# A hybrid decoder layer on one core: where the shift, scale and gate vectors are made

## The chip, the core and the metric

The kernel runs on one core of a Trainium2 chip. The metric is the device time of one launch in microseconds (us). TensorE (PE) multiplies matrices into PSUM; VectorE (DVE), ScalarE (ACT) and GpSimd (POOL) work element by element; SyncE (SP) issues nearly all DMAs. Each engine takes its own instructions strictly in the order that was fixed when the program was built, and waits on semaphores for the others. So does SP: a DMA that has to wait holds up those queued behind it.

## The reference

One decoder layer on a sequence of 1024 tokens of width 1024, in float32. A conditioning vector c gives six modulation vectors; the change is about four of them.

```python
c_act = jax.nn.silu(c)
mod = c_act @ w_ada[i] + b_ada[i]                    # (1, 6 * 1024)
sh1, sc1, g1, sh2, sc2, g2 = jnp.split(mod, 6)
h = rmsnorm(x, pre_mix_g[i]) * (1.0 + sc1) + sh1
q, k, v, u = jnp.split(h @ w_in[i], split_pts, axis=-1)
attn = sliding_window_attention(q, k, v, attn_sinks[i])
ssm = s5_mixer(u, ...)          # a scan over time, h_t = A h_{t-1} + B u_t (complex), then gelu and GLU
heads = concatenate([rmsnorm(attn, attn_out_g[i]), rmsnorm(ssm, ssm_out_g[i])])
x = x + g1 * rmsnorm(heads @ w_out[i], post_mix_g[i])
h = rmsnorm(x, pre_mlp_g[i]) * (1.0 + sc2) + sh2
x = x + g2 * rmsnorm(square(relu(h @ w_mlp_in[i])) @ w_mlp_out[i], post_mlp_g[i])
```

Shift 2 and scale 2 (sh2, sc2; numbers 3 and 4 of `mod`) are first needed after the first residual, gate 1 (number 2) just before it, and gate 2 (number 5) at the very end.

## The kernel before

The kernel is written in a tile framework. A list scheduler orders each engine's instructions when the program is built: it goes by when each could run on a simulated time line, and among those that are ready by the order in which the source emits them. Instructions given to `pin` keep their source order among themselves. From line 1354 on the order of PE is the source's own. SBUF is divided into named slots ("S3", "G2S", "B5" and so on); a new tile in a slot waits until all readers of the old one have finished.

The stages, in source order:

1. *h and u* (to line 509). The kernel makes shift 1 and scale 1 for eight column blocks, builds h for the first half of the tokens, then (line 491) for the second half with `h_step(k, 1)`, and multiplies it by the u part of w_in with `u_step`. The u weights are split in two float32r parts, `wuh` in slot B4 and `wul` in slot B5.
2. *The scan's input* (lines 507 to 517). u is transposed (`ut`) and multiplied by the state matrices (`vp`); the result is `Vs`.
3. *The scan* (lines 521 to 555 and 605 to 619). `qw`, in slot G2S, gets powers of the state's step by repeated squaring (`cpow`, with scratch in S5); `st`, in slot S7, holds temporaries. Fifteen steps of five DVE operations run within eight blocks at once, a short chain runs over the blocks, and its carries are added back into `Vs` (operand `m`, three of eight groups on POOL).
4. *Output matrices of the state space* (lines 559 to 602). POOL builds `Gs`, PE `kp`, and DMAs spread the result into `Tt`. The temporary of `Gs` shares scratch in S5 with the powers.
5. *Projections* (line 628). Six column blocks of w_in give k, v and four of q: 48 matmuls each (`pq`), with weights loaded into `wr` and split into `whi` and `wlo`. `qT` lies in slot B5, the former place of `wul`; the attention's `AB` and `PB` later take slots B0 and B1 of h.
6. *State-space output* (line 653): `yp` needs `Vs` and `Tt`; gelu gives `z`, transposed into `zh`, `zl`.
7. *Attention and GLU* (line 886): sixteen units of `scores` and `probs_t`, eight of `values`; eight GLU halves `glu`; `rms` then turns sums of squares into `ra`.
8. *Output projection, residual, MLP* (lines 915 on): `po`, then `fi` and `fo`.

`ada_block(s, b, raws)` makes 256 columns of modulation vector s. It loads 1 MB of w_ada as two raw tiles `adm` of 512 KB, in the next slots of `raws`, and `ada_parts` multiplies them by silu(c) in 16 matmuls into the one PSUM bank "D", which ACT evicts to `parts_ada`. For s = 3 and 4 (`mods2`) two one-column matmuls and small DVE operations on `sh2` and `G2` follow. For the gates (`gate_block`) three matmuls spread the row over all partitions and add the bias, DVE multiplies by the norm's gain in `gcols`, and a DMA stores the result to DRAM (`gd`), from which it is read when needed.

The generator `background` makes the eight blocks of `mods2` and then four of gate 1, all through the ring `RAWS` = S3, S6, S7, G2S, two slots a block. One block is emitted per `h_step(k, 1)` and one per `u_step` row from 4 on; `bg_steps(99)` at line 519 would emit what is left. Gate 2 has four blocks, one behind each q column block of stage 5 (line 649), all through the single slot S3.

Of the kernel before, what the change touches and what calls it, by code (L numbers as in the profile page):

```python
# [9 lines left out]
F32 = mybir.dt.float32  # L10
F32R = mybir.dt.float32r
BF16 = mybir.dt.bfloat16
AF = mybir.ActivationFunctionType
# [3 lines left out]
P = 128  # L17
# [16 lines left out]
def tile_hymba(ctx: ExitStack, tc: tile.TileContext, x, c, w_ada, b_ada, pre_mix_g, w_in,  # L34
# [4 lines left out]
    V, A, PL, T, SY = nc.vector, nc.scalar, nc.gpsimd, nc.tensor, nc.sync  # L39
# [3 lines left out]
    w_ada, w_in, w_glu, w_out = w_ada[0], w_in[0], w_glu[0], w_out[0]  # L43
# [9 lines left out]
    def nm(s):  # L53
        cnt[0] += 1
        return f"{s}_{cnt[0]}"
# [4 lines left out]
    def slot(tag, shape, dt, name):  # L60
        return sp.tile(shape, dt, tag=tag, name=nm(name))
# [3 lines left out]
    def ps(tag, name="ps"):  # L65
        return pp.tile([P, 512], F32, tag=tag, name=nm(name), bufs=NBANK[tag])
# [13 lines left out]
    def f32(ap):  # L80
        return ap.bitcast(F32)
# [7 lines left out]
    def tt(e, o, a, b, op):  # L89
        e.tensor_tensor(o, a, b, op=op)  # L90
# [34 lines left out]
    def pin(ins):  # L125
        tc.keep_in_program_order(ins)
# [47 lines left out]
    cact32 = adc[:, 2 * P:4 * P].rearrange("p (k r) -> p k r", k=KC)  # L174
# [5 lines left out]
    parts_ada = adc[:, 4 * P:8 * P].rearrange("p (e f) -> p e f", e=2)  # L180
    n_ada = [0]

    def ada_parts(srcs):


        ap_ = ps("D", "ada")
        for q in range(KC):
            c0 = 32 * (q % 4)
            T.matmul(ap_[c0:c0 + 32, 0:2 * P], cact32[:, q], srcs[q], start=q < 4, stop=q >= 4)
        n_ada[0] += 1  # L190
        o = parts_ada[:, n_ada[0] % 2]
        A.activation(o, ap_[:, 0:2 * P], AF.Copy)
        return o, ap_[:, 2 * P:4 * P]
    vps = ps("C", "vps")
    T.transpose(vps[:, 0:56], vrow[64:120], ident[64:120, 64:120])
    V.tensor_copy(vt[:, 8:64], vps[:, 0:56])
# [196 lines left out]
    for k in range(KC):  # L393
# [12 lines left out]
        part, aps = ada_parts([ad[k][q // 4][:, q % 4].rearrange("p s f -> p (s f)") for q in range(KC)])  # L406
# [20 lines left out]
        norm_x(j)  # L427


    w_ada_b = w_ada.rearrange("(q p) (s b f) -> p q s b f", p=P, s=6, f=2 * P)  # L430
    n_raw = [0]

    def ada_block(s, b, raws):

        srcs = []
        for q in range(2):
            a = slot(raws[n_raw[0] % len(raws)], [P, 4, 2 * P], F32, "adm")
            n_raw[0] += 1
            pin(SY.dma_start(a, w_ada_b[:, 4 * q:4 * q + 4, s, b, :]))
            srcs += [a[:, i] for i in range(4)]  # L440
        return ada_parts(srcs)

# [2 lines left out]
    RAWS = ("S3", "S6", "S7", "G2S")  # L445

    def mods2():
        for s in (3, 4):
            for b in range(4):
                part, o = ada_block(s, b, RAWS)  # L450
                for e in range(2):
                    T.matmul(o[:, e:e + 1], part[:, e * P:(e + 1) * P], sel[:, 0:1], start=True, stop=True)
                ks = slice(2 * b, 2 * b + 2)
                if s == 3:
                    tt(V, sh2[:, ks], o[:, 0:2], bT[:, 24 + 2 * b:26 + 2 * b], ADD)
                else:
                    tt(V, G2[:, ks], o[:, 0:2], bsc[:, 1, ks], ADD)
                    tt(V, G2[:, ks], G2[:, ks], g_mlp[:, ks], MUL)
                yield

    gd = {s: dp.tile([P, D], F32, name=f"gate{s}") for s in (2, 5)}
    gcols = slot("JK", [P, 2, 2 * P], F32, "gcols")

    def gate_block(s, b, raws):

        g = gcols[:, b % 2]
        sl = slice(2 * P * b, 2 * P * b + 2 * P)
        pin(SY.dma_start(g, (post_mix_g if s == 2 else post_mlp_g)[0, sl].partition_broadcast(P)))
        part, o = ada_block(s, b, raws)
        T.matmul(o, sel, part, start=True, stop=False)  # L470
        for e in range(2):
            r = 64 + 8 * s + 2 * b + e
            T.matmul(o[:, e * P:(e + 1) * P], ident[64:112, r:r + 1].broadcast_to([48, P]), vrow[64:112],
                     start=False, stop=e == 1)
        tt(V, g, o, g, MUL)
        pin(SY.dma_start(gd[s][:, sl], g))

    def background():
        yield from mods2()
        for b in range(4):  # L480
            gate_block(2, b, RAWS)
            yield

    bg = background()

    def bg_steps(n):
        for _ in range(n):
            next(bg, None)


    for k in range(KC):
        h_step(k, 1)
        if k % 2 == 0:
            f_group(4 + k // 2)
        bg_steps(1)
    usb = slot("B8", [P, G, 8, CI], F32, "usb")
    for j in range(8):
        if j >= 4:
            for k in range(KC):
                u_step(j, k)  # L500
            bg_steps(1)
        A.activation(usb[:, :, 7 - j, :], ups[j].rearrange("p (g c) -> p g c", g=G), AF.Copy)
    U = slot("B9", [P, G, P], F32, "U")

# [7 lines left out]
    for qg in range(8):  # L512
        vp = psR("AABABAC", "vp")
        for g in range(4):
            T.matmul(vp[:, g * P:(g + 1) * P], Ft[:, 4 * qg + g, :], U[:, 4 * qg + g, :],
                     start=True, stop=True)
        A.activation(Vs[:, 4 * qg:4 * qg + 4, 1:P], vp.rearrange("p (g n) -> p g n", g=4)[:, :, 0:P - 1], AF.Copy)

    bg_steps(99)

    qw = slot("G2S", [P, 2, 16, G], F32, "qw")
# [84 lines left out]
    for qg in range(8):  # L606
# [8 lines left out]
        o = Vv[:, gs, 1:8, :]  # L615
        m = m2[:, int(p_)].rearrange("p (g C d) -> p g C d", g=4, C=7)
# [11 lines left out]
    for m in [4, 5, 0, 1, 2, 3]:  # L628
        wr = slot("S0", [P, KC, P], F32, "wr")
        whi = slot("S1", [P, KC, P], F32R, "whi")  # L630
        wlo = slot("S2", [P, KC, P], F32R, "wlo")
        for kk in range(0, KC, 4):
            if m < 4:
                for kv in range(2):
                    SY.dma_start(wr[:, kk:kk + 4, kv * 64:kv * 64 + 64], w_in_q[:, kk:kk + 4, kv, m, :])
            else:
                SY.dma_start(wr[:, kk:kk + 4, :], w_in_k[:, kk:kk + 4, m - 4, :])
            for k2 in range(kk, kk + 4, 2):
                A.activation(whi[:, k2:k2 + 2], wr[:, k2:k2 + 2], AF.Copy)
                tt(V, wlo[:, k2:k2 + 2], wr[:, k2:k2 + 2], f32(whi[:, k2:k2 + 2]), SUB)  # L640
        dst = (qT[:, m] if m < 4 else (kT, vT)[m - 4])
        pq = [ps("A", "pq") for _ in range(2)]
        for k in range(KC):
            for h in range(2):
                mm3(pq[h], whi[:, k, :], wlo[:, k, :], hh[h][:, k, :], hl[h][:, k, :], k == 0, k == KC - 1)
        for h in range(2):
            o = dst.rearrange("p n (j l) -> p j n l", j=8)[:, 4 * h:4 * h + 4]
            A.activation(o, pq[h].rearrange("p (j n l) -> p j n l", j=4, n=8), AF.Copy)
        if m in (0, 1, 2, 3):
            gate_block(5, m, ("S3",))  # L650


    z = slot("B8", [P, 8, W], F32, "z")
    for qg in range(8):
        yp = psR("CD", "yp")
        for g in range(4):
# [3 lines left out]
                     start=False, stop=True)  # L660
# [4 lines left out]
    for f in range(4):  # L665
        for h in range(2):
# [3 lines left out]
            sl = slice(h * 512, h * 512 + 512)  # L670
# [685 lines left out]
    g = pair_first()  # L1356
# [15 lines left out]
    for p in range(NP_):  # L1372
        g = pair_in(p + 1) if p else g1
# [5 lines left out]
    t = slot("B6", [P, 4, S], F32R, "f2w2")  # L1379
    plain(NF - 4, (t[:, 0], t[:, 1]), (t[:, 2], t[:, 3]))  # L1380
    t = hs[1][:, 0].rearrange("p a b t -> p a (b t)")
# [6 lines left out]
    for ci, tag in ((NF - 2, "B1"), (NF - 1, "B7")):  # L1388
        t = slot(tag, [P, 4, S], F32R, "f2w2")
# [31 lines left out]
```

## Time and profile before

| | us |
|---|---|
| median of 3 runs | 1218.15 (1216.62 to 1220.56) |
| the profiled execution | 1216.86 |
| its span in the profile | 1215.1 |
| PE busy | 1070.1 (88%) |
| DVE busy | 913.4 (75%) |
| ACT busy | 564.4 (46%) |
| POOL busy | 559.3 (46%) |

The profile page was taken from one execution. A row of a group says: source line, engine, operation, written tile <- read tiles, shapes, count | busy us, mean ns of one | idle us of the engine just before them and what ended that. Line 90 is the helper `tt` and lines 85 to 87 are `mm3`, so those groups are told apart by their tiles. A row of the timeline is: start and length in us, engine, line, operation, tiles, shapes, count, and in brackets the idle time before it with its releaser. A row of the waits is: who waited, for whom, us in total, times, longest. A row of the windows is: the stretch, its length, each engine's busy us with its count of instructions, the granted PE clock, DMA's busy share and GB/s.

### The profile page before, as it was taken

To read this page: it belongs to the slowest core of one execution; us is meant where nothing else is said; L and a number is where in the kernel's file an instruction comes from. 1 tells how busy PE (TensorE), PEld (TensorE's weight loads), DVE (VectorE), ACT (ScalarE), POOL (GpSimd) and SP (SyncE) were. 2 spreads that over 40 slices of the span, in tenths; PEclk is the share of its full clock that TensorE was granted. 3 is DMA by queue.
4 is the path that set the end of the run, shared out by engine and by line. 5 is a ranking of instruction groups with operands and counts; after the bars stand their busy time and mean duration, and the time that the engine had idled before them with its cause. 6 is when DMAs were issued, how large, how long until landed. Compare 5 with 4: busy or idle time off the path is not lost.

```text
span 1215.1 us, 15028 instructions
## 1 busy us (share of the span) xinstructions
PE 1070.1 (88%) x5190; PEld 830.6 (68%) x5190; DVE 913.4 (75%) x1560; ACT 564.4 (46%) x1214; POOL 559.3 (46%) x476
## 2 busy tenths in 40 slices
PE   5899997474797799969999999999999999999796
PEld 3678775232655588858778777777877787787685
DVE  3350118999896435688899999999998999998956
ACT  4564221334375345647554544445454554554431
POOL 6750202401538833542454555446445545554735
PEclk9999998677898899989999999999999999999898
DMA  9944243240000422312012101211220121012135
GB/s 272 250 157 146 84 119 112 87 96 22 1 18 27 120 71 92 118 51 78 27 44 70 53 27 61 70 38 32 70 69 28 44 70 52 27 61 70 35 104 191
DMA packets 102462, 96.09 MB, mean 79 GB/s; under 512 B 22000, under 2 KB 85856, under 8 KB 102368
## 3 DMA queue, kind: packets, MB, share of 16 engines
q1 hardware_dynamic: 102048, 95.08, 25.8%
q8 instruction: 41, 0.67, 0.2%
q14 instruction: 37, 0.30, 0.1%
q10 hardware_dynamic: 240, 0.02, 0.0%
q0 software_dynamic: 96, 0.02, 0.0%
HBM read 84.48 MB, written 9.44 MB: 77 GB/s over the span
## 4 chain that ended last, share of the span: by engine, by line
PE 40%; DVE 11%; ACT 3%; issue 2%; DMA 1%; POOL 0%; POOLq 0%; DVEq 0%; SPq 0%; ACTq 0%
PE fo L85 7%; PE fi L87 7%; PE fi L85 7%; PE fi L86 7%; PE fo L86 6%; PE fo L87 6%; DVE facc L90 4%; DVE f L90 3%; DVE w L90 2%; DVE xo L1347 1%; ACT ops L1037 1%; ACT tmpc L1271 1%; DVE h2s L90 0%; ACT h2s L1037 0%; DVE ops L90 0%
## 5 line engine op out<-in xcount | busy, mean ns | idle before, releaser
L90 POOL TENSOR_TENSOR facc<-facc,tmpc 128x512 f32<-128x512 f32 x106 | 153.6, 1449 | 202.0 <-ACT tmpc L1271 194.5
L90 DVE TENSOR_TENSOR facc<-facc,fo 128x512 f32<-128x512 f32 x335 | 221.1, 673 | 12.9 <-PE fo L87 12.8
L85 PE MATMUL fo<-ops 128*128 128x512 f32 x264 | 105.0, 398 | 16.0 <-DVE facc L90 16.0
L86 PE MATMUL fo<-ops 128*128 128x512 f32 x264 | 103.1, 390 | 0.0
L87 PE MATMUL fo<-ops 128*128 128x512 f32 x264 | 103.1, 390 | 0.0
L87 PE MATMUL fi<-h,w 128*128 128x512 f32 x248 | 97.2, 392 | 6.6 <-DVE w L90 6.6
L86 PE MATMUL fi<-h,w 128*128 128x512 f32 x248 | 96.8, 390 | 0.0
L85 PE MATMUL fi<-h,w 128*128 128x512 f32 x248 | 96.8, 390 | 0.0
L90 DVE TENSOR_TENSOR w<-w1r,w 128x256 fp32r<-128x256 f32 x169 | 91.3, 549 | 1.9 <-ACT w L1037 1.9
L1037 ACT ACTIVATE ops<-f 128x512 fp32r<-128x512 f32 x66 | 41.5, 628 | 105.8 <-PE fo L86 99.9
L1116 ACT ACTIVATE f<-f 128x512 f32<-128x512 f32 x60 | 37.9, 632 | 104.1 <-DVE f L90 104.0
L1037 ACT ACTIVATE w<-w1r 128x256 fp32r<-128x256 f32 x169 | 68.8, 410 | 37.3 <-PE fi L86 24.5
L90 DVE TENSOR_TENSOR f<-fi,f 128x512 f32<-128x512 f32 x120 | 80.3, 680 | 3.6 <-PE fi L87 3.5
L90 DVE TENSOR_TENSOR ops<-f,ops 128x512 fp32r<-128x512 f32 x66 | 60.2, 912 | 25.3 <-ACT ops L1037 15.3
L90 POOL TENSOR_TENSOR w2r<-w2r,w2r 128x512 f32<-128x512 f32 x35 | 48.1, 1376 | 55.6 <-DMA w2r<-in_w_mlp_out_dram 20.5
L90 POOL TENSOR_TENSOR w1r<-w1r 128x256 f32<-128x256 f32 x60 | 67.8, 1139 | 11.5 <-DVE w L90 9.7
L85 PEld LDWEIGHTS fo<-ops 128*128 128x128 f32 x264 | 49.8, 189 | 33.3 <-DVE facc L90 23.4
L1271 ACT ACTIVATE tmpc<-fo 128x512 f32<-128x512 f32 x106 | 61.7, 582 | 11.0 <-POOL facc L90 8.8
L90 POOL TENSOR_TENSOR s<-s,pw 128x512 f32<-128x512 f32 (+1 forms) x20 | 27.4, 1375 | 83.1 <-DVE qw L90 66.3
L85 PE MATMUL fo<-h2s 128*128 128x512 f32 x128 | 50.8, 397 | 9.1 <-DVE facc L90 9.1
L87 PEld LDWEIGHTS fi<-h,w 128*128 128x128 f32 x248 | 46.8, 189 | 16.7 <-DVE w L90 7.0
L87 PEld LDWEIGHTS fo<-ops 128*128 128x128 f32 x264 | 49.7, 188 | 10.6
(361 smaller groups left out, 2965.1 us busy)
## 6 DMA issues: line engine op xcount, KB each, us to landing
adm<-in_w_ada_dram SPq DMA_DIRECT2D x32, 512.0 KB, 4.3
w2r<-in_w_mlp_out_dram SPq DMA_DIRECT2D x64, 256.0 KB, 2.7
ad<-in_w_ada_dram SPq DMA_DIRECT2D x32, 256.0 KB, 5.5
w1r<-in_w_mlp_in_dram SPq DMA_DIRECT2D x32, 256.0 KB, 3.2
w1r<-in_w_mlp_in_dram SPq DMA_DIRECT2D x16, 512.0 KB, 4.1
xn<-in_x_dram SPq DMA_DIRECT2D x8, 512.0 KB, 6.0
xin<-in_x_dram SPq DMA_DIRECT2D x8, 512.0 KB
xs<-xin SPq DMA_DIRECT2D x8, 512.0 KB, 2.6
```

Of the source, the lines that this page charges most:

```text
L85: T.matmul(ps, lh, rh, start=first, stop=False)
L86: T.matmul(ps, lh, rl, start=False, stop=False)
L87: T.matmul(ps, ll, rh, start=False, stop=last)
L90: e.tensor_tensor(o, a, b, op=op)
L1037: A.activation(hi, src, AF.Copy)
L1116: A.activation(o, o, AF.Relu)
L1271: A.activation(tmpc, p_, AF.Copy)
L1347: V.scalar_tensor_tensor(xin[:, sl], ag_[:, j % 4, sl], r_, xin[:, sl], op0=MUL, op1=ADD)
```

## The change

Three things are done. First, `bg` is `mods2` alone, and two of its blocks instead of one are emitted per `h_step(k, 1)`, so that all eight stand in the first four of eight steps; the call in the u rows goes. Secondly, gate 1 and gate 2 are both made by a new generator `gates`, all eight blocks emitted at line 519, behind `Vs` and ahead of `qw`; their raw tiles are the four quarters of a tile of their own, `graw`, in slot B5, between `wul` and `qT`. The blocks of gate 2 in the projection loop go. Thirdly, the DMAs of the gates are no longer pinned; those of `mods2` still are. `ada_parts` takes its width from its operands; it is 256 columns as before.

```diff
-    def ada_block(s, b, raws):
+    def ada_block(s, cols, raws, ld):
         srcs = []
         for q in range(2):
-            a = slot(raws[n_raw[0] % len(raws)], [P, 4, 2 * P], F32, "adm")
+            a = raws[n_raw[0] % len(raws)]
+            if isinstance(a, str):
+                a = slot(a, [P, 4, 2 * P], F32, "adm")
             n_raw[0] += 1
-            pin(SY.dma_start(a, w_ada_b[:, 4 * q:4 * q + 4, s, b, :]))
+            ld(SY.dma_start(a, w_ada_s[:, 4 * q:4 * q + 4, s, cols]))
...
     def mods2():
         for s in (3, 4):
             for b in range(4):
-                part, o = ada_block(s, b, RAWS)
+                part, o = ada_block(s, slice(2 * P * b, 2 * P * b + 2 * P), RAWS, pin)
...
-        pin(SY.dma_start(g, (post_mix_g if s == 2 else post_mlp_g)[0, sl].partition_broadcast(P)))
-        part, o = ada_block(s, b, raws)
+        SY.dma_start(g, (post_mix_g if s == 2 else post_mlp_g)[0, sl].partition_broadcast(P))
+        part, o = ada_block(s, sl, raws, lambda i: i)
...
         tt(V, g, o, g, MUL)
-        pin(SY.dma_start(gd[s][:, sl], g))
-
-    def background():
-        yield from mods2()
-        for b in range(4):
-            gate_block(2, b, RAWS)
-            yield
-
-    bg = background()
+        SY.dma_start(gd[s][:, sl], g)
+
+    def gates():
+        t = slot("B5", [P, 4, 4, 2 * P], F32, "graw")
+        for s in (2, 5):
+            for b in range(4):
+                gate_block(s, b, [t[:, i] for i in range(4)])
+                yield
+
+    bg = mods2()
...
         h_step(k, 1)
         if k % 2 == 0:
             f_group(4 + k // 2)
-        bg_steps(1)
+        bg_steps(2)
...
             for k in range(KC):
                 u_step(j, k)
-            bg_steps(1)
...
+    bg = gates()
     bg_steps(99)
...
-        if m in (0, 1, 2, 3):
-            gate_block(5, m, ("S3",))
```

More of the change, by code (lines that the diff above doesn't have):

```diff
@@ L183, in ada_parts @@
     def ada_parts(srcs):
+        n = 1
+        for d in srcs[0].shape[1:]:
+            n *= d
         ap_ = ps("D", "ada")
@@ L188, in ada_parts @@
             c0 = 32 * (q % 4)
-            T.matmul(ap_[c0:c0 + 32, 0:2 * P], cact32[:, q], srcs[q], start=q < 4, stop=q >= 4)
+            T.matmul(ap_[c0:c0 + 32, 0:n], cact32[:, q], srcs[q], start=q < 4, stop=q >= 4)
         n_ada[0] += 1
-        o = parts_ada[:, n_ada[0] % 2]
-        A.activation(o, ap_[:, 0:2 * P], AF.Copy)
-        return o, ap_[:, 2 * P:4 * P]
+        o = parts_ada[:, n_ada[0] % 2, 0:n]
+        A.activation(o, ap_[:, 0:n], AF.Copy)
+        return o, ap_[:, 2 * P:2 * P + n]
     vps = ps("C", "vps")
@@ L427, in tile_hymba @@
         norm_x(j)
-    w_ada_b = w_ada.rearrange("(q p) (s b f) -> p q s b f", p=P, s=6, f=2 * P)
+    w_ada_s = w_ada.rearrange("(q p) (s f) -> p q s f", p=P, s=6)
     n_raw = [0]
-    def ada_block(s, b, raws):
+    def ada_block(s, cols, raws, ld):
         srcs = []
         for q in range(2):
-            a = slot(raws[n_raw[0] % len(raws)], [P, 4, 2 * P], F32, "adm")
+            a = raws[n_raw[0] % len(raws)]
+            if isinstance(a, str):
+                a = slot(a, [P, 4, 2 * P], F32, "adm")
             n_raw[0] += 1
-            pin(SY.dma_start(a, w_ada_b[:, 4 * q:4 * q + 4, s, b, :]))
+            ld(SY.dma_start(a, w_ada_s[:, 4 * q:4 * q + 4, s, cols]))
             srcs += [a[:, i] for i in range(4)]
```

## The prediction

> **What bounds the kernel now.** I read the page first: the span, the 40 slices, and the chain that ended last.
>
> ```profile
> span 1215.1 us, 15028 instructions
> DVE  3350118999896435688899999999998999998956
> GB/s 272 250 157 146 84 119 112 87 96 22 1 18 27 120 71 92 118 51 78 27 44 70 53 27 61 70 38 32 70 69 28 44 70 52 27 61 70 35 104 191
> PE 40%; DVE 11%; ACT 3%; issue 2%; DMA 1%; POOL 0%; POOLq 0%; DVEq 0%; SPq 0%; ACTq 0%
> ```
>
> The chain's shares add to 57%: it was followed back only to about 522 us, in the MLP. It says nothing of the first 425 us, where the change lies. In the DVE row a slice is 30.4 us; slices 4 to 6 (91 to 182 us) are nearly empty, slices 7 to 11 full. So I cut that stretch into windows.
>
> ```profile
> core 0: us, PE busy (x) PEld busy (x) DVE busy (x) ACT busy (x) POOL busy (x), PEclk, DMA share, GB/s
> 105.00:121.00 16.00, 15.68 (x159) 13.56 (x159) 0.88 (x6) 9.95 (x19) 0.00 (x0) 1.00 0.42 141
> 121.00:187.00 66.00, 65.61 (x343) 48.16 (x341) 8.50 (x24) 13.64 (x35) 7.07 (x4) 1.00 0.42 117
> 187.00:326.00 139.00, 85.11 (x509) 52.90 (x507) 135.29 (x305) 42.42 (x127) 41.04 (x25) 0.74 0.23 59
> 326.00:425.00 99.00, 81.64 (x431) 55.08 (x432) 63.91 (x130) 53.83 (x133) 64.21 (x52) 0.91 0.17 50
> 425.00:545.00 120.00, 112.59 (x513) 92.68 (x512) 73.46 (x92) 63.97 (x139) 52.58 (x49) 0.97 0.25 85
> 545.00:1215.00 670.00, 624.37 (x2713) 507.24 (x2713) 594.81 (x911) 326.56 (x667) 335.32 (x262) 0.98 0.19 60
> ```
>
> From 121 to 187 PE is full and DVE works 8.50 of 66 us. From 187 to 326 it is reversed: DVE 135.29 of 139 us, PE slack at a granted clock of 0.74. Two stages that could lie side by side run one after the other. The timeline says why.
>
> ```profile
> 121.01 0.60 ACT L517 ACTIVATE Vs<-vp 128x508 f32<-128x508 f32 x1 [0.17 <-PE vp L515]
> 186.37 0.64 PE L189 MATMUL ada<-adm,adc 128*32 128x256 f32 x8
> 187.08 0.19 DVE L522 COPY qw<-pw 128x64 f32<-128x64 f32 x1 [9.58 <-DMA wr<-in_w_in_dram]
> 201.64 0.39 PE L87 MATMUL pq<-h1h,wlo 128*128 128x512 f32 x1
> 325.00 0.62 DVE L90 TENSOR_TENSOR Vs<-Vs,m 128x448 f32<-128x448 f32 x1
> POOL s L90 <- DVE qw L90: 66.3, 1, 66.3
> ```
>
> The scan's input Vs is complete at 121.61. Its first operation, the copy into qw, starts at 187.08. The row names a DMA into wr, but qw lives in slot G2S, and that slot is the last raw tile of the fourth gate-1 block, whose matmuls end at 187.01, 0.07 us earlier. So **the scan waits 65 us for a gate that nobody needs yet**, and POOL's second product for Gs waits 66.3 us behind the same powers (they share scratch in S5). The scan's last addition is at 325.
>
> **The change part by part.** *The slot wait goes.* Shift and scale 2 still use S3, S6, S7 and G2S, but are done while h is built; the gates read B5. G2S and S7 are then free before Vs is complete, and the powers and the scan may start at about 122. What is late next is DVE itself, so I count its work. Scan and powers, from the groups of 187 to 326:
>
> ```profile
> L90 DVE TENSOR_TENSOR st<-Vs,qw 64x256 f32<-64x256 f32 (+1 forms) x45 | 39.2, 871 | 0.8
> L90 DVE TENSOR_TENSOR Vs<-Vs,st 128x256 f32<-128x256 f32 x30 | 20.3, 677 | 0.3
> L90 DVE TENSOR_TENSOR m<-st,qw 128x448 f32<-128x448 f32 x10 | 13.9, 1389 | 0.3
> L90 DVE TENSOR_TENSOR Vs<-Vs,m 128x448 f32<-128x448 f32 x10 | 10.4, 1037 | 0.3
> L90 DVE TENSOR_TENSOR s<-qw 128x32 f32<-128x32 f32 (+3 forms) x8 | 2.3, 282 | 0.2
> L757 DVE TENSOR_REDUCE sm<-AB 128x4 f32<-128x512 f32 x7 | 4.8, 682 | 0.0
> ```
>
> The four large groups are 83.8 us. The powers are 24 products and sums at about 0.28 us, 7 us. The chain over the eight blocks adds some 10. So about 100 us of scan must fit between 122 and the end of PE's projections; the other 35 us of the 135.29 are attention (seven of the sixteen units' second reductions are in this window).
>
> DVE work after 121 is 8.5 + 135.3 + 63.9 = 207.7 us. The change removes none. The powers (7 us) can run ahead of 121, where DVE has 15 idle us in 16, and so can the last update of G2 (0.6). One thing is added: contention with POOL.
>
> ```profile
> 241.00 1.78 DVE L90 TENSOR_TENSOR st<-Vs,qw 128x256 f32<-128x256 f32 x3
> 212.19 5.83 DVE L90 TENSOR_TENSOR st<-Vs,qw 128x256 f32<-128x256 f32 x3
> 213.61 1.77 POOL L90 TENSOR_TENSOR s<-s,pw 128x896 f32<-128x896 f32 x1
> 215.46 2.19 POOL L90 TENSOR_TENSOR Gs<-Gs,s 128x896 f32<-128x896 f32 x1
> ```
>
> The same three scan products take 1.78 us alone and 5.83 beside two POOL products of 1.77 and 2.19: DVE lost 4.05 us to 3.96 us of POOL, all of it. POOL's first four Gs products (7.07 us, 121 to 187) now have no scan beside them and will have: bounds 0 and +7.1; I take 7.1, since that row lost all. The Trainium skill, "SBUF — State Buffer", "Who interferes with whom", says that a VectorE operation with two SBUF inputs and a GpSimd operation that reads SBUF hold one port pair in turn, the loser blocked for the whole instruction; the trace agrees (4.05 against 3.96). By the rule the sum has the 7.1 wherever the two meet, without it the term could be anything down to 0; this is the one place where a rule speaks against the change.
>
> *Shift and scale 2, two blocks a step.* 8 blocks as before. A block is 16 matmuls, a small eviction on ACT and one or two tiny DVE operations.
>
> ```profile
> 129.79 1.07 PE L189 MATMUL ada<-adm,adc 128*32 128x256 f32 x16
> 69.51 44.59 SPq L439 DMA_DIRECT2D adm<-in_w_ada_dram  x12
> ```
>
> Seven are done by 121; only the eighth (1.07 us and four 128x1 matmuls, 1.6 in all) moves ahead of Vs: +1.6. SP holds those loads back for free raw tiles (12 issues in 44.59 us), with DMA share 0.42: there is room. Nothing behind them on SP is urgent, as wr for the next column block is issued after its predecessor was split.
>
> *The gates.* Eight blocks behind Vs instead of four among the projections, one at their end and three in the attention.
>
> ```profile
> 144.18 0.59 PE L470 MATMUL ada<-adc 128*128 128x256 f32 x2
> 144.70 0.71 PE L473 MATMUL ada<-adc,ident 48*128 48x128 f32 x4
> 145.34 0.50 PE L86 MATMUL pq<-h1l,whi 128*128 128x512 f32 x1
> adm<-in_w_ada_dram SPq DMA_DIRECT2D x32, 512.0 KB, 4.3
> PE ada L189 <- DVE gcols L90: 10.8, 3, 4.1
> PE ada L189 <- DMA adm<-in_w_ada_dram: 8.4, 2, 7.0
> ```
>
> A block costs PE 1.0 + 1.2 = 2.2 us. Four more before the projections end, less the 1.6: PE is through at about 202 + 7 = 209, still ahead of the scan's end (122.6 + 93 + 7.1 + DVE's other 8.5 us there = 231), so it costs nothing; its cover is 22 us, and past that each us costs one. The raw loads can start when u has read B5, at 105: 16 x 0.5 MB at the page's best rate, 272 GB/s, is 31 us, then a block's tail: done by 145 to 165. qT, which takes B5 next, is written by the third of six column blocks, which take (202 - 121)/6 = 13.5 us each, so not before 160 and with the gates between them nearer 170. The waits on SP for a gate product hold up the loads queued behind; PE queues in order behind a block whose tile is late. In the old order the last four blocks, through one raw slot, cost PE 10.8 + 8.4 = 19.2 us. With four tiles I take 1 us a block, 8, on the path; bounds 0 and 38 (19.2 for every four).
>
> *The end of the stage.* After the scan come gelu, GLU and the rest of attention.
>
> ```profile
> 408.62 1.87 PE L852 MATMUL rp<-ones,sss 128*128 128x1 f32 x8 [7.33 <-POOL sss L90]
> 422.11 3.47 POOL L90 TENSOR_TENSOR ra<-ra,nhalf 128x8 f32<-128x8 f32 x2
> ```
>
> From 326 to 425 it is the GLU chain through POOL that ends last, and DVE idles 99 - 63.9 = 35.1 us. With attention's 35 us now in it, some of that idle time is filled: between none and all; I take half, 17.5 left.
>
> **The sum.** 121 + 1.6 + (207.7 - 7.6 + 7.1) + 3.7 (DVE's idle time within 187 to 326) + 17.5 + 8 = 359 against 425: 66 us earlier. The MLP behind it (790 us) has the same work in the same PE order. The profiled execution took 1216.86 us (span 1215.1), 1.3 below the median shown: 1216.86 - 66 = **1151**.
>
> **Rivals.**
> 1. *The tail fills completely*: no idle in it and no gate waits: 359 - 25.5 = 333, 92 us gained, 1125. For it: GLU can now start while up to nine more units of attention are still to come (7 of 16 are left at 326 now). Against: ACT, PE and DVE would all be near full there.
> 2. *The gates hold the scan on DVE.* A gate product waits in DVE's queue and the scan behind it. If each block goes alone (4.3 us to land, 2.2 PE, 0.4 eviction, 0.4 product), eight from 106 end at 165; scan at 165, not 187: 22 us, and with half the tail filled 39: 1178 to 1195. For it: they are emitted ahead of the scan. Against: the queue order is made from ready times and the scan is ready first.
> 3. *The scan doesn't start earlier*, as something else holds G2S or S7: 1217. Against: the 0.07 us between the matmul's end and qw.
> 4. *Slower*: PE, in order, stalls at every gate block for its raw tile, and the projections, scores and everything behind them wait. Scan and projections then end at 209 + 8s for a stall of s; attention and tail after that need DVE's 35.3 + 63.9 and 17.5 idle = 117 us. That is later than 425 from 209 + 8s = 308, s = 12.4 us a block; the longest single stall in the rows above is 7.0. At s = 14 it gives 1230.
>
> **How the numbers follow.** Forecast 0.56 (own range 1136 to 1178: tail idle from 10 to 35, gate waits 0 to 19); rival 1 0.18 (1118, if the 7.1 is 0 too, to 1136); rival 2 0.16 (1178 to 1195); rival 3 0.04; rival 4 0.06. The range of 8 in 10 is 1125 to 1191: it leaves out 0.07 of rival 1, 0.04 of rival 2 and all of 3 and 4. Faster by over 0.3% (3.7 us, about what a measurement can tell from no change) 0.90, within it 0.04, slower 0.06.
>
> **What would show it.** Right: qw's copy before 125, the four gcols products of gate 2 done by 150, no POOL wait on qw over 10 us; Vs's last addition at 225 to 240; scores starting at about 210; the first 128x8 power of ra at 345 to 365; 425 to the end unchanged in length. Wrong: PE idle before L189 above 20 us in all, a gcols product in DVE's row with scan operations waiting behind it, or the GLU chain ending as late after the scan as now (97 us).

## The result, and the profile after

| | before | after |
|---|---|---|
| median, us | 1218.86 (4 runs, 1216.62 to 1220.56) | 1188.45 (4 runs, 1187.53 to 1189.09) |
| ratio | | 0.9751, 95% interval 0.9732 to 0.977 |
| the profiled execution / its span | 1216.86 / 1215.1 | 1187.53 / 1185.6 |
| first operation of the scan | 187.1 | 130.7 |
| last addition of the scan ends | 325.6 | 241.6 |
| last projection matmul ends | 202.0 | 267.1 |
| first score matmul | 227.2 | 272.1 |
| first and second evaluation of `ra` on DVE | 421.0, 423.2 | 387.9, 401.9 |

The kernel is 30 us faster; the forecast was 66. The windows of the changed kernel, cut where its stages now change (columns as before):

```profile
core 0: us, PE busy (x) PEld busy (x) DVE busy (x) ACT busy (x) POOL busy (x), PEclk, DMA share, GB/s
121.00:131.00 10.00, 10.00 (x59) 7.62 (x58) 1.63 (x5) 2.76 (x8) 7.07 (x4) 1.00 0.14 51
131.00:242.00 111.00, 79.51 (x468) 56.28 (x467) 106.57 (x192) 22.89 (x45) 36.98 (x22) 0.80 0.43 105
242.00:267.00 25.00, 25.00 (x122) 20.76 (x121) 2.38 (x8) 4.89 (x12) 0.49 (x1) 1.00 0.16 49
267.00:393.00 126.00, 106.31 (x610) 64.38 (x609) 107.60 (x254) 74.65 (x229) 61.88 (x51) 0.95 0.16 43
513.00:1185.00 672.00, 624.84 (x2713) 507.22 (x2713) 597.29 (x912) 326.51 (x667) 337.09 (x263) 0.98 0.19 60
```

The two stages that lay one after the other now overlap: from 131 to 242 DVE is full and PE works 79.51 of 111 us. But then a hole opens that the profile before did not have: from 242 to 267 PE is full and DVE has 2.38 us of work. Attention cannot start, because the projections are not done. In the timeline, the points where the stage turns:

```profile
130.68 0.20 DVE L528 COPY qw<-pw 128x64 f32<-128x64 f32 x1 [5.04 <-PE ada L192]
239.43 1.07 PE L192 MATMUL ada<-graw,adc 128*32 128x256 f32 x16 [0.29 <-DVE gcols L90]
240.93 0.62 DVE L90 TENSOR_TENSOR Vs<-Vs,m 128x448 f32<-128x448 f32 x1
266.73 0.39 PE L87 MATMUL pq<-h1h,wlo 128*128 128x512 f32 x1
```

The scan starts 56 us earlier and ends 84 us earlier, but the last raw tile of the gates is read at 239 to 240.5 and the last projection ends at 267. The waits between 130 and 270 us name what PE, and then DVE, stood for, and the rows of `gcols` and `qT` show the rhythm:

```profile
PE ada L192 <- DVE gcols L90: 24.0, 5, 10.1
DVE AB L701 <- PE pq L87: 10.3, 1, 10.3
PE pq L87 <- DVE wlo L90: 5.2, 2, 3.1
```
```profile
152.99 0.43 DVE L90 TENSOR_TENSOR gcols<-ada,gcols 128x256 f32<-128x256 f32 x1
174.03 0.42 DVE L90 TENSOR_TENSOR gcols<-ada,gcols 128x256 f32<-128x256 f32 x1
...
243.42 0.42 DVE L90 TENSOR_TENSOR gcols<-ada,gcols 128x256 f32<-128x256 f32 x1 [1.86 <-PE ada L478]
```
```profile
L654 ACT ACTIVATE qT<-pq x8: 585/600/629, 240.9 to 267.5; 128x512 f32<-128x512 f32 x8
L744 PE MATMUL sc<-kT,qT x128: 272/376/480, 272.1 to 356.0; 64*128 64x256 f32 x112, 64*128 64x128 f32 x16
```

A gate block goes from PE to ACT, back to PE, to DVE, and only then may PE begin the next one in the single bank D. Each product takes 0.42 us, but it stands in DVE's order among the scan's operations, so that a product comes 4 to 21 us after the one before. The first evictions of `qT` stand at 240.9, right behind the last reader of B5, 240.5: they waited for the slot. PE's last `pq` matmul before that ended at 210.5; until 242 its order held gate blocks and `yp`.

### The profile page after: what moved, and what is told of

The parts are those of the page before. It is cut to its first block, busy times and chain, and to the rows that moved or that the text cites. A ratio compares the mean times of both kernels' runs of the same rounds, so it can differ in the third digit from the quotient of the medians.

```text
span 1185.6 us, 15026 instructions
## 1 busy us (share of the span) xinstructions
PE 1060.5 (89%) x5190; PEld 825.1 (70%) x5190; DVE 923.1 (78%) x1560; ACT 560.7 (47%) x1213; POOL 554.7 (47%) x476
## 4 chain that ended last, share of the span: by engine, by line
PE 40%; DVE 12%; ACT 3%; issue 3%; POOL 1%; DMA 0%; DVEq 0%; POOLq 0%; ACTq 0%
PE fo L85 7%; PE fi L87 7%; PE fi L85 7%; PE fi L86 7%; PE fo L86 6%; PE fo L87 6%; DVE facc L90 4%; DVE f L90 3%; DVE w L90 2%; DVE xo L1351 1%; ACT ops L1041 1%; DVE ops L90 1%; ACT tmpc L1275 1%; DVE h2s L90 0%; ACT h2s L1041 0%
## 5 line engine op out<-in xcount | busy, mean ns | idle before, releaser
L90 POOL TENSOR_TENSOR w2r<-w2r,w2r 128x512 f32<-128x512 f32 x35 | 48.2, 1380 | 55.8 <-DMA w2r<-in_w_mlp_out_dram 20.7
L85 PEld LDWEIGHTS fo<-ops 128*128 128x128 f32 x264 | 49.8, 189 | 33.4 <-DVE facc L90 23.5
L90 POOL TENSOR_TENSOR w1r<-w1r 128x256 f32<-128x256 f32 x60 | 67.1, 1128 | 12.1 <-DVE w L90 9.7
L87 PEld LDWEIGHTS fo<-ops 128*128 128x128 f32 x264 | 49.8, 189 | 10.6
L86 PEld LDWEIGHTS fo<-ops 128*128 128x128 f32 x264 | 49.9, 189 | 9.5
```

The lines of the kernel that those rows point to most:

```text
L85: T.matmul(ps, lh, rh, start=first, stop=False)
L86: T.matmul(ps, lh, rl, start=False, stop=False)
L87: T.matmul(ps, ll, rh, start=False, stop=last)
```

## The experiments

Four theories. **Theory 1**: `qT`'s wait for slot B5 costs the time. **Theory 2**: the gates' round trips over DVE's order cost it. **Theory 3**: DVE's splits of the projection weights (`wlo`) and the contention with POOL cost it, the gates little. **Theory 4** came after the first eight runs: it is the gates' work on PE itself, since work that PE doesn't get done inside the scan is done behind it.

| run | time, us | ratio to before (95%) | PE idle, 131 to 242 | scan ends | last projection ends | first score | span less first score |
|---|---|---|---|---|---|---|---|
| the changed kernel | 1188.45 | 0.9751 (0.9732 to 0.977) | 31.5 | 241.6 | 267.1 | 272.1 | 913.5 |
| e1_s35 | 1194.63 | 0.9809 (0.9788 to 0.983) | 20.7 | 273.3 | 242.1 | 257.4 | 936.2 |
| e2_pool | 1186.87 | 0.9749 (0.9733 to 0.9765) | 35.4 | 242.7 | 266.8 | 271.8 | 914.2 |
| e3_none (no gates) | 1164.08 | 0.9559 (0.9543 to 0.9575) | 29.8 | 244.9 | 232.4 | 247.0 | 914.0 |
| e4_bef3 | 1194.86 | 0.9823 (0.9793 to 0.9853) | 30.8 | 242.9 | 250.1 | 255.1 | 938.5 |
| e5_clean | 1186.17 | 0.9739 (0.9724 to 0.9753) | 30.3 | 242.4 | 258.2 | 264.8 | 919.9 |
| e6_wlo | 1193.82 | 0.9804 (0.9789 to 0.9818) | 38.9 | 243.8 | 273.4 | 278.4 | 913.8 |
| e7_none_wlo (no gates) | 1165.25 | 0.9567 (0.9551 to 0.9583) | 35.6 | 243.1 | 236.9 | 248.4 | 914.6 |
| e8_all | 1185.97 | 0.9741 (0.9726 to 0.9755) | 37.5 | 247.3 | 258.8 | 267.0 | 916.8 |
| e9_pework (no products) | 1181.48 | 0.9693 (0.9679 to 0.9708) | 33.6 | 240.7 | 259.0 | 266.1 | 914.1 |
| e10_best | 1178.03 | 0.9665 (0.9648 to 0.9681) | 35.4 | 243.2 | 252.6 | 259.2 | 917.6 |
| e11_act | 1182.76 | 0.9705 (0.9689 to 0.972) | 32.0 | 242.4 | 257.9 | 264.5 | 917.7 |
| e12_order | 1181.79 | 0.9709 (0.9693 to 0.9725) | 37.5 | 242.2 | 252.4 | 259.2 | 920.1 |
| e13_none_order (no gates) | 1165.7 | 0.9571 (0.9556 to 0.9586) | 36.0 | 242.1 | 235.1 | 247.5 | 916.8 |
| e14_both_orders | 1174.43 | 0.9636 (0.9622 to 0.9649) | 18.0 | 242.8 | 222.5 | 248.3 | 924.4 |
| e15_last_block | 1191.76 | 0.978 (0.9764 to 0.9797) | 33.2 | 230.9 | 272.7 | 277.7 | 914.9 |
| e16_all_orders | 1175.92 | 0.9649 (0.9634 to 0.9664) | 23.8 | 220.1 (POOL's share 247.5) | 243.5 | 252.0 | 920.2 |

The five right-hand columns are from each run's profile. The runs without gates or without products leave out part of the layer, so that they bound what a cause can cost and are no kernels to use. The table already holds the main finding: in 14 of 17 rows the kernel ends 913 to 921 us behind its first score, and the first score comes 2 to 9 us behind the later one of the scan's end and the projections' end. (The three others are e1, with a scan that went on behind the first score, e4, with gate blocks behind it, and e14.) So the question is what makes the projections end late.

**e1 and e5: the slot.**

```diff
-        t = slot("B5", [P, 4, 4, 2 * P], F32, "graw")
+        t = [slot(k, [P, 4, 2 * P], F32, "graw") for k in ("S3", "S5")]
```
and in e5 besides
```diff
-    m2 = slot("S5", [P, 2, 448], F32, "m2")
+    m2 = [st[:, 0:448], slot("PW", [P, 448], F32, "m2")]
```

> The changed kernel with one edit: the gates' raw w_ada tiles go through slots S3 and S5 (two tiles, one block deep) instead of B5, so that nothing of the gates stands in qT's slot. Theory 1 (the evictions of qT's first two row blocks wait until 240.5 us for the last matmul that reads B5, and hold PE's four A banks meanwhile): those evictions come before 225 us, the projections end at 225 to 245 us instead of 266.9, and the kernel takes 1160 to 1172 us, against 1188 for the changed kernel. Theory 2 (the gates' round trips over DVE's in-order queue set the end of the projections, whichever slot the raw tiles have): no more than 8 us is won, 1180 to 1190 us, and PE still waits some 25 us for gate products. Theory 3 (DVE and POOL slow each other and DVE's splits of the projection weights come late; the gates matter little): 1183 to 1190 us.

> The changed kernel with the gates' raw tiles in slots S3 and S5, as in e1, and with the scan's last product tile m2 no longer in S5 (DVE's half stands in free columns of st, POOL's half in the slot of pw), because in e1 the scan's last operations waited for S5 and the scan ended at 262 us instead of 241. It is the test of theory 1 without that side effect. Theory 1 (qT's wait for B5 sets the end of the projections): the scan ends at 238 to 245 us, the projections before 245, the first scores at 245 to 252, and the kernel takes 1165 to 1176 us. If qT's slot costs nothing because other waits end at the same time: 1184 to 1190 us, with the projections again at 260 or later.

e1 was confounded: the scan's last products wanted S5 and the scan ended 32 us later, at 273.3. e5 mends that. `qT`'s first eviction comes at 185.7 instead of 240.9, so the slot wait is gone, and the kernel wins 2.3 us. **Theory 1 falls**; the projections still end at 258.2. PE's waits in e5 say why:

```profile
PE ada L192 <- DVE gcols L90: 17.7, 4, 5.7
PE pq L87 <- DVE wlo L90: 13.4, 3, 5.8
```

24.0 and 5.2 have become 17.7 and 13.4, about the same sum.

**e2 and e3: the product off DVE; no gates.** In e2 ACT copies a block's sum to a buffer in S3 and POOL multiplies; in e3 `bg = gates()` goes.

```diff
-        tt(V, g, o, g, MUL)
+        go = gout[0][:, b % 2]
+        A.activation(go, o, AF.Copy)
+        tt(PL, g, go, g, MUL)
```

> The changed kernel with one edit: a gate block's product is no longer DVE's. ACT copies the 128x256 sum out of PSUM and POOL multiplies it; the raw tiles stay in B5. Theory 2: a block no longer waits behind the scan's operations on DVE, the eight blocks are through by 175 to 200 us instead of 243, qT finds B5 free, and the kernel takes 1140 to 1160 us. Theory 1 alone (the slot counts, the round trip doesn't): the same if the blocks get done early, so this run tells the cause of the late blocks; if they still end after 230 us behind POOL's Gs products, 1183 to 1195 us. Theory 3: 1183 to 1190 us however early the gates are done.

> The changed kernel without the eight gate blocks: the two gate rows are loaded from post_mix_g and post_mlp_g as they are (both gate products are left out). It is the ceiling for everything that the gates cost between 130 and 270 us. Theories 1 and 2: projections end at 200 to 215 us, attention starts before the scan ends or right with it, 1135 to 1155 us. Theory 3: 1178 to 1188 us.

Without the gates 24.4 us are won (1188.45 to 1164.08): that is all that the gates cost. It lies outside every range: theories 1 and 2, with 1155 at the most, expected more, and theory 3, with 1178 at the least, less. With the products on POOL 1.6 us are won, where theory 2 expected at least 28: the products alone are not the cause. The waits, first of e2, then of e3:

```profile
PE pq L87 <- DVE wlo L90: 25.1, 2, 12.8
```
```profile
PE pq L87 <- DVE wlo L90: 27.7, 4, 12.3
```

The wait for gate products is gone in both, and a wait for the splits has its length. DVE has one order, and it holds the scan; whatever PE needs from DVE next comes when its turn among the scan's operations comes. From here on this is theory 2.

**e4: the slot G2S alone.** In the kernel before, gate 1 loads into `("S3", "S5")` instead of `RAWS`; nothing else is touched.

> The kernel before with one edit: the four gate 1 blocks load into slots S3 and S5 and no longer into S3, S6, S7 and G2S; gate 2 stays beside the projections through S3, every load stays pinned to its place in the queue, and the shift and scale blocks stay one to a step. It takes from the scan the slot on which it waited and moves nothing else. If the slot G2S was all that held the scan (the forecast's first step): the qw copy comes at 130 to 140 us instead of 187, the scan ends at 240 to 250 us, and the kernel takes 1155 to 1190 us. If the order of the loads or the gate 1 products hold the scan as well, it takes 1200 us or more and the qw copy comes after 160 us.

The qw copy comes at 131.0 and the scan ends at 242.9, as expected for the slot; the time, 1194.86, is 5 us above the range. 22.9 of the some 30 us come from freeing that one slot. The rest of the change, all gates ahead of the scan, is worth some 6 us more (1188.45).

**e6 and e7: the splits on POOL**, with and without gates.

```diff
-                tt(V, wlo[:, k2:k2 + 2], wr[:, k2:k2 + 2], f32(whi[:, k2:k2 + 2]), SUB)
+                tt(PL, wlo[:, k2:k2 + 2], wr[:, k2:k2 + 2], f32(whi[:, k2:k2 + 2]), SUB)
```

> The changed kernel with one edit: the 24 subtractions that make wlo (128x256 each) go to POOL instead of DVE. Theory 2 in its present form (during the scan all that PE needs from DVE comes late, since it stands behind the scan's operations in DVE's order; with one such need taken away PE stops at the next): the waits for gate products stay at 20 to 30 us, qT still waits for B5 until 230 us or later, and the kernel takes 1178 to 1190 us. Theory 3 (the splits hold PE, the gates matter little): 1160 to 1172 us, projections done by 235. Against the edit: POOL and DVE slow each other, which can make the scan up to 10 us longer.

> Both gates left out (the two gate rows loaded as they are) and the 24 subtractions on POOL: then PE needs nothing from DVE between 135 us and the end of the scan. Theory 2: PE's idle time between 131 and 212 us falls from 24 us (in e3) to under 8, and the projections end at 205 to 215 us as the forecast had it. If the projections' end set the start of attention in e3, the kernel takes 1140 to 1152 us. If the end of the scan sets it (the score tables of attention are made on DVE behind the scan), the first scores stay at 240 to 250 us and the time at 1154 to 1166 us.

**Theory 3 falls** as a cause by itself: e6 is 5 us slower than the changed kernel (and 4 above theory 2's range). PE's waits, of e6 and then of e7:

```profile
PE ada L192 <- DVE gcols L90: 35.0, 5, 13.2
```
```profile
PE yp L661 <- DVE Vs L90: 26.3, 1, 26.3
```

In e6 the wait went back to the gate products and grew. e7 has neither gates nor splits on DVE, and PE still stood: the planner had put `yp` matmuls, which need the scan's result, ahead of the last projections. PE's idle time did not fall under 8 us as I had expected, and the projections ended at 236.9, not at 205 to 215. The first score, 248.4, follows the scan's end, 243.1, as in e3; so here the projections don't matter, and the time is that of e3.

**e8 and e11: more of the gates off DVE.** e8 is e5 with the product on POOL and the splits on POOL; a block then takes both halves of `gcols`, so that two blocks can't overlap there. e11 is e5 with no product at all in the block: ACT copies the sum, the store follows, and POOL multiplies the gain in after the gate row has been read back.

> All gates computed, with three edits together: raw tiles in S3 and S5 with m2 moved as in e5, the gate product on POOL after a copy by ACT, and the 24 subtractions on POOL. Theory 2: PE waits for nothing of DVE until the scan's end, the eight blocks are through by 215 us, the projections by 235, and the kernel takes 1158 to 1172 us, within 10 us of the run without gates (1164). If the contention of POOL and DVE eats it: the scan ends after 250 us and the time is 1176 to 1190 us.

> As the run before in this call, but with the splits' subtractions and dsT left on DVE: only the gate blocks are freed of DVE and POOL (PE, ACT, PE, ACT, store), with raw tiles in S3 and S5. Theory 2: the gate waits go but the waits for the splits take their place, as in e2 and e3 (25 to 28 us), so that the time stays at 1178 to 1187 us. If the gate round trips alone were the cause: 1166 to 1174 us.

They took 1185.97 and 1182.76 us; e8 missed theory 2's range by 14, e11 lies in it. In e8 the blocks stood on POOL behind `m`, which waited 29.6 us for the scan, and PE waited 17.8 us for `wlo` and 12.6 for `Gs`, both on POOL; in e11 PE waited 31.8 us for `wlo` on DVE.

**e9: the PE work without the round trips.**

```diff
-        A.activation(o, ap_[:, 0:n], AF.Copy)
+        if ev:
+            A.activation(o, ap_[:, 0:n], AF.Copy)
...
-        tt(V, g, o, g, MUL)
-        SY.dma_start(gd[s][:, sl], g)
```

> The changed kernel with the gates' raw loads and all their matmuls left in place, but with nothing hung on them: the copy of the partial sums by ACT, the product and the store are gone, the second matmuls read an old copy, and the two gate rows are loaded as they are (both gate products are left out). It keeps the 19 us or so that the eight blocks take of PE and takes away the round trips over ACT and DVE. Theory 2 (the round trips behind the scan cost the 24 us between this and the run without gates): 1162 to 1170 us, and the projections end before 240. Theory 4, new (PE is full from the scan's end at 241 to 300 us, so whatever gate work PE does inside the scan pushes projection work of the same length behind it, with or without round trips): 1180 to 1187 us.

1181.48, in theory 4's range. **Of the 24.4 us of the gates, 7.0 went with the round trips and 17.4 stayed with their loads and matmuls.** The last raw tile is read at 195 instead of 240, so B5 is free too, and still the projections end at 259.0. PE waits as long as before, now for `wlo`:

```profile
PE pq L87 <- DVE wlo L90: 30.9, 3, 15.3
```

In PE's order the gate blocks do not stand where it waits: PE idles 33.6 us, against 29.8 in e3, with the gates' 18 us of matmuls to do besides. The loads were not taken out by themselves, but no DMA is among PE's waits here.

**e10, e12, e14: taking the scan out of everybody's order.** e10 is e11 with the splits on POOL and `dsT` copied by ACT. e12 and e14 add an order without a semaphore: the first `yp` behind the last projection on PE, and the first `m` behind the last split on POOL (with that loop moved behind the projections in the source; `last_pq` and `last_wlo` are the last of their kind, `im` the first product of the loop).

```diff
-            T.matmul(yp[:, g * P:(g + 1) * P], U[:, gg, :], Tt[:, gg, :], start=True, stop=False)
+            ym = T.matmul(yp[:, g * P:(g + 1) * P], U[:, gg, :], Tt[:, gg, :], start=True, stop=False)
+            if gg == 0:
+                tc.add_manual_dep(ym.ins, last_pq.ins.name,
+                                  mybir.DependencyInfo(mybir.DependencyClass.NoSync, mybir.DependencyReason.DATA),
+                                  reason="projections first")
...
+            if qg == 0 and a_ is hb:
+                tc.add_manual_dep(im.ins, last_wlo.ins.name,
+                                  mybir.DependencyInfo(mybir.DependencyClass.NoSync, mybir.DependencyReason.DATA),
+                                  reason="splits first")
```

> All gates computed, with nothing of them or of the projection weights behind the scan on DVE, or behind POOL's wait for the scan: raw tiles in S3 and S5 and m2 moved as in e5; ACT copies the gate sums out of PSUM and they are stored without their factor, which POOL multiplies in after the two gate rows have come back; the 24 subtractions of the splits on POOL; the small copy dsT, for which POOL waited 11 us, on ACT. Theory 2: PE's idle time from 131 to 242 us falls from 31 us to under 15, the first scores come at 245 to 252, and the kernel takes 1164 to 1174 us. Theory 4: PE's idle time falls too, and the time with it by about as much, 1165 to 1176; if PE's idle time does not fall because the planner's order puts scan results (yp) ahead of the last projections, 1180 to 1188.

> As e10, with one edit more: the first yp matmul is ordered behind the last projection matmul on PE (in e10 the planner had put two yp groups ahead of the last projections, and PE stood 29.7 us waiting for the scan's Vs). Theory 4 with its reason (inside the scan PE always finds something in its order that waits for the scan, and the work so kept back is done behind the scan at the rate of a full PE): PE's idle time from 131 to 241 us falls from 35 us to under 15 and the rest of it is real want of work, the projections end at 215 to 230, the first scores come at 245 to 250, and the kernel takes 1156 to 1168 us. If PE is not what sets the time behind the scan: 1174 to 1180 us.

> As e12, with POOL's share of the scan's last products (m2) moved behind the projections in the program and ordered behind the last of the splits on POOL: in e12 PE stood 30.0 us waiting for a split that stood on POOL behind an m2 product, which waited for the scan. Now nothing in PE's, POOL's or ACT's order waits for the scan before projections and gates are through. Theory 4 with its reason: PE's idle time before the end of the projections falls under 10 us, the projections and gates end at 220 to 235, first scores at 246 to 252, and the kernel takes 1158 to 1170 us, near the run without gates (1164 to 1166). If PE is not what sets the time behind the scan, or the scan grows by more than 8 us because POOL works beside it for longer: 1174 to 1182 us.

PE's longest waits inside the scan, of e10, e12 and e14 in this order, with e14's window:

```profile
PE yp L669 <- POOL Vs L90: 29.7, 1, 29.7
```
```profile
PE pq L87 <- POOL wlo L90: 30.3, 2, 30.0
```
```profile
PE sc L755 <- DVE AB L723: 12.1, 1, 12.1
PE pq L85 <- ACT whi L633: 4.9, 2, 3.6
PE yp L677 <- DVE Vs L90: 3.7, 1, 3.7
```
```profile
131.00:242.00 111.00, 93.05 (x549) 68.25 (x547) 106.91 (x162) 30.54 (x63) 55.08 (x43) 0.91 0.44 114
```

In e10 it was PE's own order, in e12 POOL's: a split stood behind an `m` that waited for the scan. e10's PE idled no less (35.4 us), and its 1178.03 lies between theory 4's two ranges; e12 was 3.8 us slower than e10 and missed both of its ranges. Only in e14, with both orders put right, does the 30 us wait end and not come back under another name: PE's idle time is 18.0 us, and the last 6 of these, from 236 on, already belong to a wait of 12.1 for attention's tables, with all projections and gates done. The projections end at 222.5, the first score comes 5.5 us behind the scan, and the kernel takes 1174.43 us: **14 us or 1.2% less than the changed kernel**. That is 4 us outside theory 4's range and just inside the other one. So these runs show that the scan, through the orders of PE and POOL, kept the projections back (they end 30 us earlier than in e10 and e12), and that I overrated what it is worth.

**e13: the same without gates.**

> As e7 (both gates left out, splits on POOL), with dsT copied by ACT and the yp matmuls ordered behind the projections: then nothing in PE's order waits for the scan before the projections are through, which is what the forecast took for granted. Projections end at 200 to 215 us. If the forecast's tail was right once its cover is real: 1148 to 1156 us. If the end of the scan sets attention's start whatever PE has done (its tables stand behind the scan on DVE): first scores at 245 to 250, as in e3, and 1156 to 1164 us.

1165.7, no better than e3. Only the first `yp` was tied, and others again stood ahead of the last projections (`yp` waited 32.8 us, the projections ended at 235.1), so the premise wasn't met. What can be read is that the first score follows the scan's end by 5.4 us (2.1 in e3, 5.3 in e7, 5.5 in e14).

**e15 and e16: an earlier scan.** The eighth shift and scale block loads into S3 and S6, in the changed kernel and in e14.

```diff
-                part, o = ada_block(s, slice(2 * P * b, 2 * P * b + 2 * P), RAWS, pin)
+                part, o = ada_block(s, slice(2 * P * b, 2 * P * b + 2 * P), ("S3", "S6") if (s, b) == (4, 3) else RAWS, pin)
```

> The changed kernel with one edit: the eighth shift and scale block loads into S3 and S6 instead of S7 and G2S, which the scan needs (DVE waited from 121.9 to 130.7 us for them, its Vs having been ready at 121.3). It tests the forecast's first step, which put the scan's start at 122. The scan starts at 121 to 124 and ends at 231 to 236 us. If the time behind the scan is DVE's, as the forecast had it: all of 8 to 9 us is won, 1179 to 1181. If PE's work behind the scan sets it (theory 4): the same work stands behind an earlier end, and 0 to 5 us are won, 1183 to 1189.

> The same edit on the kernel of e14, whose PE had 12 us of want behind the projections, waiting for attention's tables behind the scan: there the end of the scan is the bound, so an earlier start is won nearly whole. Theory 4: 1164 to 1169 us against 1174; if the eighth block's loads, now one deep, hold PE ahead of the scan: 1172 us or more.

In e15 the scan starts at 113.7 and ends 10.7 us earlier, and the kernel is 3.3 us **slower**. Of e15, and then of e16:

```profile
113.72 0.20 DVE L528 COPY qw<-pw 128x64 f32<-128x64 f32 x1 [3.10 <-PE ada L192]
```
```profile
242.79 4.78 DVE L715 TENSOR_SCALAR AB<-ident 128x128 bf16<-128x128 f32 x8 [22.71 <-PE pq L87]
```

In e15 the last shift and scale blocks now had their DVE operations among the scan's (PE waited 13.6 us for them), and the projections ended at 272.7. In e16 the same wait was the longest of PE's:

```profile
PE ada L192 <- DVE G L90: 21.7, 2, 14.3
```

DVE's part of the scan is over at 220.1, DVE then stands 22.71 us for PE's projections, and POOL's share, ordered behind the splits, ends at 247.5; 1175.92 against 1174.43. Neither run won anything. So the end of the scan on DVE was not the bound in either; but as new waits came in with the edit, neither run says what an earlier scan would be worth with PE's work done in time.

## Why the forecast was wrong

**What bounds the kernel** was right. The 65 us for slot G2S were the wait to remove: e4 removes it alone and wins 22.9 us.

**The scan's start** was off by 8.7 us: 130.7, not 122. I let two blocks per step and the freed slots move the eighth block ahead; its matmuls came at 129.54, as before (129.79), and it still used S7 and G2S, so the scan waited for it. Its last raw tile was asked for at 113.4 and these loads land in 3.7 to 5.7 us; but PE is busy in all of 121 to 131, and its order held `pq` matmuls ahead of the block. Emitting a block earlier did not move it. The powers and the last update of `G2` (7.6 us in the forecast), which were to run ahead of 121, ran behind 130.7 too.

**The scan's length** came out right by luck: 110.9 us from the qw copy to the last addition, against 109 in the forecast (231 less 122). The 110.9 hold the powers, which end at 139.6 and which the forecast had outside; the rest took 102. POOL's lock was there. The Trainium skill's rule ("SBUF — State Buffer", "Who interferes with whom") fits these rows again:

```profile
146.01 6.45 DVE L90 TENSOR_TENSOR st<-Vs,qw 128x256 f32<-128x256 f32 x3
```
```profile
145.56 2.28 POOL L90 TENSOR_TENSOR Gs<-Gs,s 128x896 f32<-128x896 f32 x1
147.92 1.91 POOL L90 TENSOR_TENSOR s<-s,pw 128x896 f32<-128x896 f32 x1
149.91 2.18 POOL L90 TENSOR_TENSOR Gs<-Gs,s 128x896 f32<-128x896 f32 x1
```

Three products that take 1.78 us alone took 6.45, 4.67 us more. POOL was busy for nearly all of that stretch.

**The step that failed** is the one on the gates: "PE is through at about 202 + 7 = 209, still ahead of the scan's end ..., so it costs nothing; its cover is 22 us", and with it "done by 145 to 165" for the raw tiles. The projections ended at 267.1, 58 us later and 25 us behind the scan; the raw tiles were read until 240.5. I had taken PE's finish of the kernel before, 202, and added work to it. But until 187 PE had had DVE nearly to itself (8.50 us busy in 66). With the scan in that place, every split and every product that PE needs stands in an order beside 107 us of DVE work.

The traces say where the 58 us went, if each PE instruction is counted until the next one starts and weighted with the granted clock. From 121 to its last projection PE took 146.1 us, against 81.0 before. The gates' own work is 7.4 us of the difference, about as forecast (7). The rest stands nowhere in the 209: 31 us of idle time, for the waits; 14.4 us because the granted clock was 0.50 in 44 of the 111 us (PE lost nothing to the clock before); 9.9 us of `yp`, which the planner put ahead of the last projections; and 3 us of `kp` and `vt`, which had come later before. Once PE has lost so much, its work is no longer hidden: e9 shows 17.4 us for loads and matmuls that I priced at nothing. The clock also tells e10 from e5: over the same stretch PE idled 35.4 and 31.1 us, but lost 2.1 and 14.5 us to the clock, and the projections of e10 ended 5.6 us earlier.

**qT and slot B5.** "Not before 160 and nearer 170" was wrong about when the slot came free (240.5), yet e5 shows that it cost only 2.3 us.

**The sum.** Put the end of the stage at 393: what lies behind it takes 792.6 us, against 790.1 behind 425 before. That is 34 us behind the forecast's 359, and the sum's own terms say where they went.

| DVE, us | forecast | measured |
|---|---|---|
| idle ahead of the scan | 1.6 | 8.4 (121 to 131) |
| idle within it | 3.7 | 4.4 (131 to 242) |
| idle for the gates | 8 | 22.6 (242 to 267) |
| idle behind it | 17.5 | 18.4 (267 to 393) |
| work from 121 on | 207.2 | 218.2 |

Two terms failed, by some 14 us each: the gates (22.6 for 8) and the start (6.8 of idle time, and the 7.6 of powers and update, which make up most of the 11 us of work). The half that I took for the tail's idle time came out right, though it was a guess. e3 agrees: the gates cost 24.4 us, of which the sum had 8, and some 20 us more were missing without any gates; there the scan ends at 244.9 and not at 231. And in e15 the powers start at 113.7 and the scan ends at 230.9, as forecast, while the projections end at 272.7 and the kernel takes 1191.76 us: there an earlier scan was worth nothing, as PE's order kept the projections back. What it would be worth otherwise stays open, since e15 and e16 had new waits of their own. Also open is why e14 needs 8.7 us more than e13; 7.6 of these lie behind the first score.

The two evaluations of `ra`, 2 us apart before, were 14 apart after (387.9 and 401.9), since attention now ends last.

**The rivals.** The time lies in rival 2's 1178 to 1195, and that rival alone carried my range up to 1191; this was luck, as the way was another: the gates did not hold the scan on DVE, the scan held them. Rival 4's mechanism, PE stalled at the gate blocks, was the right one at a smaller size: 24.0 us in five stalls, for the product and not for the raw tile. Among the signs that I named, "PE idle before L189 above 20 us" came true (24.0, now line 192), and so did a late GLU chain (the last `ra` 160 us behind the scan; I had named 97). Of the signs on the other side, the qw copy missed 125 by 6 us, the scan's end 240 by 2, the first power of `ra` 365 by 23 (388.1); the scores, foreseen at 210, came at 272.1, and the products of gate 2, due by 150, came from 221 to 244.

## What to carry to other kernels

When a long chain is moved beside work that used to have the engine to itself, don't take that work's old finish: list every operation that it needs from the busy engine, and from any engine whose order holds something that waits for the chain, and expect one wait to take the place of another until all of these orders are clear. Sum the work of every engine over the whole stage; where two are within a few per cent, the time is neither sum (here PE's 222 and DVE's 219 us of work from 131 to 404 took 273). Add to a wait on PE what the clock costs behind it. And look for the one event behind which the rest of the kernel has a fixed length (here the first score, with 913 to 921 us behind it in 14 of 17 kernels): a change in the stage is worth what it moves that event.

## What the runs showed of the hardware

A wait on PE can cost more than its length. In e7, after a gap of 1.46 us and some narrow matmuls, the 128x512 matmuls started 0.43 us apart for 3.4 us, and then 0.23 apart:

```profile
149.98 0.63 PE L85 MATMUL pq<-h1h,whi 128*128 128x512 f32 x1
150.40 0.63 PE L86 MATMUL pq<-h1l,whi 128*128 128x512 f32 x1
...
152.96 0.59 PE L86 MATMUL pq<-h1l,whi 128*128 128x512 f32 x1
153.39 0.40 PE L85 MATMUL pq<-h1h,whi 128*128 128x512 f32 x1
153.62 0.40 PE L86 MATMUL pq<-h1l,whi 128*128 128x512 f32 x1
```

Eight matmuls at 0.20 us too much are 1.6 us. The granted clock was 0.50 from 150.0 to 153.4 us, and 1.00 just before and just after. From 131 to 242 us its mean was 0.80 in the changed kernel and 0.91 in e14, where PE waits less; weighted with PE's busy time, 14.4 and 6.6 us of PE's work were lost to it. I had priced PE's work at its full rate. The Trainium skill, "TensorE: Matmul & The Clock Gate", Part 1, says that PE runs at half its rate until it has been busy for about 3.4 us; the spacing in these rows agrees. What lowered the clock here the rows do not settle: the longest gap ahead was 1.46 us, and the narrow matmuls beside it (16 columns) may count for it.
